# Weight-quarter sums moved between the stages of a decoder layer, a drain of GpSimd behind the last of them, and mLSTM scores made for two heads in turn

## The chip, the cores and the metric

The kernel runs on one core of one Trainium2 chip. The metric is the device time of one execution in microseconds, as the median of several runs, compared on the same chip with runs of the kernel before. A profile is one execution of its own, taken by the hardware profiler.

TensorE (PE, with PEld for its weight loads) multiplies, VectorE (DVE), ScalarE (ACT) and GpSimd (POOL) work on tiles, and SyncE (SP) issues nearly all transfers. Each engine takes its instructions in the order in which they stand in the program, and waits on semaphores where one needs the result of another engine. GpSimd issues transfers too: those that add to what stands at the destination.

## The reference

One decoder layer on 512 tokens of width 1024, all in float32, in three steps, each between two norms and with a residual:

```python
x = x + 0.5 * rms_norm(swiglu_ffn(rms_norm(x, norm_pre[0]), ffn1_w_in, ffn1_w_out), norm_post[0])
x = x + rms_norm(token_mixer(rms_norm(x, norm_pre[1]), ...), norm_post[1])
x = x + 0.5 * rms_norm(swiglu_ffn(rms_norm(x, norm_pre[2]), ffn2_w_in, ffn2_w_out), norm_post[2])

def swiglu_ffn(x, w_in, w_out):            # inner width 2816
    gate, up = jnp.split(x @ w_in, 2, axis=-1)
    return (jax.nn.silu(gate) * up) @ w_out
```

The token mixer makes one combined projection and runs two recurrences on its columns, an HGRN2 with four heads of 128 and an mLSTM with four heads of 64 (keys and queries) and 128 (values), each with a norm and a gate, and then an output projection. The scores of an mLSTM head are, chunk by chunk,

```python
D = jnp.where(causal, b[..., :, None] - b[..., None, :] + ic[..., None, :], -jnp.inf)
P = jnp.einsum("bhtd,bhsd->bhts", qc, kc) * jnp.exp(D - m_t[..., None])
```

## The kernel before

Every product of the large matrices is made of three products of rounded parts: a weight tile `raw` of 512 KB is loaded by SP (`load`, L242), ScalarE writes its rounded part and VectorE the rest (`split`, L279 and L281), and TensorE multiplies high by high, high by low and low by high. Both FFNs save products with a scheme of seven products of quarters in place of eight (`prod` and `after` for the first matrix, `quartered` and `common` for the second). The scheme needs sums of quarters of the weights. For the first matrix they are made on chip (L295). For 13 of the 22 blocks of the second matrix they are made in DRAM ahead of time, and loaded like weights.

Such a sum is made by `sums_ahead(f, h, k2)`, for FFN `f` ("f1" or "f2"), output half `h` and block `k2`, in steps of a generator. The first step puts three copies on SP (L868 to L870), behind the latest weight load. The next three steps issue one accumulating DMA each from GpSimd (L873). Each of these three reads what the one before wrote, so it waits for its landing. `make_sums` starts one new sum, if `sums_due` has left any, and moves each open one a step on. It is called from places in the other work:

- first FFN: sums of "f1", in `ffn_in`, at every fifth product behind the fourteenth, and in the first half of `ffn_out`
- mixers: the eight sums of "f2", half 0 (blocks 2 to 9), at the four `job_f` of the convolution's columns and at each weight pull of the `job_t` of "hi" and "mv", twelve calls
- second FFN: the five sums of "f2", half 1 (blocks 2, 4, 3, 6, 8), in `ffn_in` at every tenth product behind the fourteenth, and in the first half of `ffn_out` behind each second block (`if half == 0 and n % 2`)

In `ffn_out` each output half runs over eleven blocks; between the halves `post0` takes the squares of half 0 and its statistics, some of them on GpSimd (`rms`, L437).

The mixers interleave the recurrences with the big projections: a queue of jobs (`job_f`, `job_t`, `job_rows`) holds the matmuls of the projections, and `fill(n)` takes n pieces from it between the small steps. The order of each engine's instructions is fixed when the program is built; a scheduler may move instructions within the bounds of their needs. In the built program GpSimd's DMAs of the eight mixer sums stand in one run, ahead of the clearing of the mLSTM state (L1548) and of the four causal selects (L1515).

`mlstm_scores` makes the scores of the four heads. For a head, `mlstm_head` takes the row maxima by a matmul with a selector (`neg_m`, L1489), VectorE and ScalarE make the decay `e` (L1511 to L1514), GpSimd sets to zero what isn't causal (L1515), TensorE multiplies keys and queries, four chunks into one PSUM bank (L1523), and VectorE multiplies both into `pT` (L1525). Heads 0 and 2 lie in the lower 64 rows of their tile, heads 1 and 3 in the upper ones. Behind them come two more `neg_m`, transposes of the keys (L1570) and the state updates (L1585). PSUM has eight banks; four of them hold the running projection.

At the end of the program each engine closes with a drain, and a barrier of all engines ends the kernel (L1861).

Of the kernel before, what the change touches and what calls it, by code (L numbers as in the profile page):

```python
# [11 lines left out]
ALU = mybir.AluOpType  # L12
# [6 lines left out]
NT = T // P  # L19
# [9 lines left out]
NH = 4  # L29
# [55 lines left out]
PLACES, LATER = {2: 1, 4: 2, 6: 0, 8: 3}, {7: (2, 3)}  # L85

AGAIN, ROWS = (10,), (18, 19, 20, 21)
EVERY = 5, 10

# [25 lines left out]
class Layer:  # L117
# [663 lines left out]

    def ffn_in(self):

        self.sums_due("f2" if self.second else "f1", (1,) if self.second else (0, 1))
        for n, (p, t) in enumerate(ORDER2[len(HEADS2) :] if self.second else ORDER[len(HEADS) :]):
            if n > 14 and n % EVERY[self.second] == 0:
                self.make_sums()
            with self.behind(*(self.c22 if p == "p3" and self.second else ())):
                self.feed()
            self.c22 = []  # L790
            self.lag()
            self.prod(p, t)
            self.after(p, t)
            if t == PAIRS - 1 and p in ("p3", "p7"):
                self.hs.append(self.h_tile(len(self.hs)))
        self.feed()
        self.lag()
# [64 lines left out]
    def sums_ahead(self, f, h, k2):  # L862

        nc, to = self.nc, self.sums_of[f, h, k2]
        w = (self.ffn1_w_out, self.ffn2_w_out)[f == "f2"][0]
        q = w[k2 * 2 * P : (k2 + 1) * 2 * P, h * 512 : (h + 1) * 512].rearrange("(k p) (c f) -> p k c f", p=P, f=QUARTER)
        with self.behind(self.loaded):
            nc.sync.dma_start(to[:, 0], q[:, 0, 1])  # L868
            nc.sync.dma_start(to[:, 1], q[:, 1, 0])
            nc.sync.dma_start(to[:, 2:], q[:, 1])  # L870
        yield
        for a, b, v in ((0, 2, q[:, 0, :1].broadcast_to([P, 2, QUARTER])), (2, 3, to[:, :1]), (3, 4, to[:, 2:3])):
            nc.gpsimd.dma_start(to[:, a:b], v, accum_op=ALU.add)  # L873
            yield

    def sums_due(self, f, halves):
        self.ahead, self.making = deque(k for k in self.sums_of if k[0] == f and k[1] in halves), []

    def make_sums(self):

# [4 lines left out]
    def ffn_out(self, gpost_row, scale, after, trans, head):  # L885
# [81 lines left out]

        with self.behind(*([self.loaded] if self.second else [])):
            g = self.gain("gpost", gpost_row)
        n = 0  # L970
        for half in range(2):
            C = [[self.ps() for _ in range(2)] for _ in range(2)]
            M, T, left = None, None, len(QUARTERED[half])
            for m, k2 in enumerate(OUT[half][: PAIRS - LAST * half]):
# [24 lines left out]
                    self.after("p4", PAIRS - 1)  # L999
                self.lag()  # L1000
            if half == 0:
                ys = [self.post0(pieces(C, i), g, scale) for i in range(NT)]
                self.holes()
        ws = []
# [41 lines left out]
    def job_f(self, name, then):  # L1046

        w, ps = self.pull(), self.ps()
        if name[0] == "c":
            self.make_sums()  # L1050
        for k in range(ND):
            self.in_k(ps, w, k, [(0, HALF), (HALF, T)])
# [374 lines left out]
    def job_rows(self):  # L1427

        ps = self.ps()[:100]
        for k in range(ND):  # L1430
            for n in range(2):
                for m in range(2):
# [71 lines left out]
    def mlstm_head(self, h):  # L1504

        nc = self.nc
# [14 lines left out]
        for c in range(NT):  # L1521
            s = slice(c * P, (c + 1) * P)
            nc.tensor.matmul(sc[:, s], self.qk[o : o + 64, 2 + h // 2, s], self.qk[o : o + 64, h // 2, s], start=True, stop=True)  # L1523
        yield
        nc.vector.scalar_tensor_tensor(self.pT[:, h, :], sc, 0.125, e, op0=ALU.mult, op1=ALU.mult)  # L1525
        yield

    def mlstm_scores(self, mc):
# [2 lines left out]
        self.nend = mc.tile([P, NH, NT], F32, name="nend")  # L1531
        self.pT = mc.tile([P, NH, T], F32, name="pT")
        H = [self.mlstm_head(h) for h in range(NH)]
        next(H[0])
        for h in range(NH):
            if h + 1 < NH:
                next(H[h + 1])
            self.fill(3)
            next(H[h])
            next(H[h])  # L1540
        w = mc.tile([P, NT, NH], F32, name="w")
        nc.vector.tensor_tensor(w, self.aT, self.nend.rearrange("p h c -> p c h"), op=ALU.add)
        nc.scalar.activation(w, w, AF.Exp)
# [127 lines left out]
    def mixer(self):  # L1671
        nc, tc = self.nc, self.tc
        self.got, self.jobs = set(), deque()
        self.sums_due("f2", (0,))
        with tc.tile_pool(name="ma", bufs=1) as ma:
            self.vh = ma.tile([P, NT, NH, P], F32, name="vh")
            self.vm = ma.tile([P, NT, NH, 129], F32, name="vm")
# [187 lines left out]
```

## Time and profile before

| | |
|---|---|
| median of 3 runs | 937.68 us (935.62 to 940.22) |
| profiled execution | 936.0 us, its span 934.3 us |
| granted TensorE clock | 0.998 |
| busy: PE, DVE, ACT, POOL | 922.8, 759.2, 521.5, 179.5 us |
| first FFN, mixers, second FFN | about 0 to 340, 340 to 600, 600 to 934 us |
| mixer sums on GpSimd | 394.95 to 484.44 us |

In the rows below a time is in us from the start of the span. A row of a timeline gives start, duration, engine, line, operation, what is written and read, the number of instructions merged, and in brackets how long the engine stood idle before it and what ended that. PEld is the weight load of TensorE, which runs beside the matmuls. A row of the waits reads: engine, tile, line, what it waited for, us in total, times, longest. A row of a window gives its bounds and length, then the busy us and the number of instructions of PE, PEld, DVE, ACT and POOL, the granted clock, the busy share of the DMA engines and GB/s. The busy time of a pipelined matmul overlaps the next one, so the number of matmuls in a window tells more than its busy time.

### The profile page before, as it was taken

To read this page: it belongs to the slowest core of one execution; us is meant where nothing else is said; L and a number is where in the kernel's file an instruction comes from. 1 tells how busy PE (TensorE), PEld (TensorE's weight loads), DVE (VectorE), ACT (ScalarE), POOL (GpSimd) and SP (SyncE) were. 2 spreads that over 40 slices of the span, in tenths; PEclk is the share of its full clock that TensorE was granted. 3 is DMA by queue.
4 is the path that set the end of the run, shared out by engine and by line. 5 is a ranking of instruction groups with operands and counts; after the bars stand their busy time and mean duration, and the time that the engine had idled before them with its cause. 6 is when DMAs were issued, how large, how long until landed. Compare 5 with 4: busy or idle time off the path is not lost.

```text
span 934.3 us, 18295 instructions
## 1 busy us (share of the span) xinstructions
PE 922.8 (99%) x7435; PEld 887.7 (95%) x7435; DVE 759.2 (81%) x980; ACT 521.5 (56%) x751; POOL 179.5 (19%) x250
## 2 busy tenths in 40 slices
PE   9999999999999999999999999999999999999996
PEld 7999999999999999998888887899999999999996
DVE  6899988889887786698766555799899889988883
ACT  7646455557566457956523345594445545756641
POOL 3531112211111045222230310313010010100001
PEclk9999999999999999999999999999999999999999
DMA  9255778766996234477742125253376556467522
GB/s 315 70 152 143 187 206 194 193 147 160 241 276 215 81 98 123 121 176 160 170 87 63 45 90 175 88 166 93 97 192 171 150 159 198 132 193 224 175 74 91
DMA packets 116494, 142.28 MB, mean 152 GB/s; under 512 B 7189, under 2 KB 89657, under 8 KB 116410
## 3 DMA queue, kind: packets, MB, share of 16 engines
q1 hardware_dynamic: 101562, 126.95, 43.8%
q0 software_dynamic: 14560, 13.64, 11.2%
q8 instruction: 58, 0.95, 0.4%
q10 hardware_dynamic: 288, 0.52, 0.2%
q14 instruction: 26, 0.21, 0.1%
HBM read 138.99 MB, written 29.36 MB: 180 GB/s over the span
## 4 chain that ended last, share of the span: by engine, by line
PE 54%; DVE 5%; issue 2%; DMA 2%; POOL 1%; ACT 1%; DVEq 0%; POOLq 0%; ACTq 0%
PE ps L602 14%; PE ps L928 7%; PE ps L532 6%; PE ps L920 5%; PE ps L185 5%; PE ps L187 5%; PE ps L186 5%; DVE w L281 2%; PE ps L1342 2%; DMA raw<-in_ffn_w_in_dram 2%; DVE raw L295 1%; PE ps L347 1%; POOL raw L295 1%; PE ps L542 1%; PE ps L1523 0%
## 5 line engine op out<-in xcount | busy, mean ns | idle before, releaser
L279 ACT CAST w<-raw 128x1024 fp32r<-128x1024 f32 x244 | 249.6, 1029 | 195.8 <-PE ps L602 85.5
L281 DVE TENSOR_TENSOR w<-raw,w 128x1024 fp32r<-128x1024 f32 x244 | 297.5, 1222 | 32.8 <-ACT w L279 31.5
L602 PE MATMUL ps<-xq,w 128*128 128x256 f32 x2016 | 237.3, 277 | 0.0
L602 PEld LDWEIGHTS ps<-xq,w 128*128 128x128 f32 x2016 | 232.9, 188 | 0.1
L602 PE MATMUL ps<-sq,w 128*128 128x256 f32 x1512 | 178.2, 276 | 2.2 <-DVE ps L621 1.8
L602 PEld LDWEIGHTS ps<-sq,w 128*128 128x128 f32 x1512 | 174.3, 188 | 3.2 <-issue 2.0
L295 DVE TENSOR_TENSOR raw<-raw,raw 128x1024 f32<-128x1024 f32 x72 | 89.8, 1251 | 11.8 <-DMA raw<-in_ffn_w_in_dram 10.3
L920 PE MATMUL ps<-w,hs 128*128 128x256 f32 x768 | 91.2, 276 | 0.0
L920 PEld LDWEIGHTS ps<-w,hs 128*128 128x128 f32 x768 | 88.9, 188 | 0.0
L185 PE MATMUL ps<-w,xq 128*128 128x512 f32 x192 | 78.0, 407 | 0.1
L928 PE MATMUL ps<-w,hs 128*128 128x256 f32 x624 | 75.0, 276 | 0.0
L186 PE MATMUL ps<-w,xq 128*128 128x512 f32 x192 | 74.9, 391 | 0.0
L187 PE MATMUL ps<-w,xq 128*128 128x512 f32 x192 | 74.8, 391 | 0.0
L928 PEld LDWEIGHTS ps<-w,hs 128*128 128x128 f32 x624 | 72.7, 188 | 0.0
L532 PE MATMUL ps<-xq,w 128*128 128x256 f32 x480 | 55.7, 277 | 0.0
L532 PEld LDWEIGHTS ps<-xq,w 128*128 128x128 f32 x480 | 54.9, 188 | 0.5 <-issue 0.5
L814 ACT CAST hs<-hf 128x1024 fp32r<-128x1024 f32 x34 | 35.8, 1053 | 34.2 <-PE ps L928 22.3
L815 DVE TENSOR_TENSOR hs<-hf,hs 128x1024 fp32r<-128x1024 f32 x34 | 41.5, 1221 | 11.9 <-ACT hs L814 11.5
L873 POOL DMA_DIRECT2D f1sums<-f1sums x26 | 22.8, 879 | 111.7 <-DMA f1sums<-in_ffn_w_out_dram 53.1
L185 PEld LDWEIGHTS ps<-w,xq 128*128 128x128 f32 x192 | 36.1, 188 | 8.5 <-issue 0.9
L187 PEld LDWEIGHTS ps<-w,xq 128*128 128x128 f32 x192 | 36.0, 188 | 8.1 <-DVE xq L354 0.3
L873 POOL DMA_DIRECT2D f2sums<-in_ffn_w_out_dram x13 | 17.3, 1333 | 137.3 <-DMA f2sums<-in_ffn_w_out_dram 137.3
(262 smaller groups left out, 1201.6 us busy)
## 6 DMA issues: line engine op xcount, KB each, us to landing
raw<-in_ffn_w_in_dram SPq DMA_DIRECT2D x98, 512.0 KB, 4.9
raw<-in_ffn_w_out_dram SPq DMA_DIRECT2D x44, 512.0 KB, 4.5
raw<-in_w_mix_in_dram SPq DMA_DIRECT2D x28, 512.0 KB, 4.1
raw<-f1sums SPq DMA_DIRECT2D x13, 512.0 KB, 7.5
raw<-f2sums SPq DMA_DIRECT2D x13, 512.0 KB, 4.5
raw<-in_w_mix_out_dram SPq DMA_DIRECT2D x8, 512.0 KB, 4.3
f1sums<-in_ffn_w_out_dram SPq DMA_DIRECT2D x26, 128.0 KB, 4.4
f1sums<-in_ffn_w_out_dram SPq DMA_DIRECT2D x13, 256.0 KB, 5.5
```

What stands on the lines that cost most here:

```text
L185: mm(ps, sh, mh, start=start, stop=False, **kw)
L186: mm(ps, sh, ml, start=False, stop=False, **kw)
L187: mm(ps, sl, mh, start=False, stop=stop, **kw)
L279: nc.scalar.copy(hi, raw)
L281: self.low = nc.vector.tensor_tensor(lo, raw, hi.bitcast(F32), op=ALU.subtract)
L295: (nc.vector if late else nc.gpsimd).tensor_tensor(o, o, c, op=ALU.add)
L532: mm(ps[:, u0:u1], w[:, a, k, :], self.xop(k, b, u0, u1), start=k + n + m == 0, stop=k == ND - 1 and n == 2, skip_group_check=True,)
L602: self.nc.tensor.matmul(ps[:, c], wb[b][:, k, v], left[d][:, k, :], start=first and a + n + k == 0, stop=n == 2 and k == KH - 1, skip_grou ...
L815: self.nc.vector.tensor_tensor(lo, src, hi.bitcast(F32), op=ALU.subtract)
L873: nc.gpsimd.dma_start(to[:, a:b], v, accum_op=ALU.add)
L920: mm(out, a[kk][:, i * P : (i + 1) * P], w[:, b, kk, QUARTER * v : QUARTER * (v + 1)], start=begin and c == kk == n == 0, stop=kk == 1 and ...
L928: mm(ps[:, QUARTER * c : QUARTER * (c + 1)], A[a][:, c], B[b], start=begin and c == n == 0, stop=n == 2, skip_group_check=True,)
```

## The change

Five edits go together:

- `sums_due` takes a number instead of halves. The mixers now make the first ten sums of "f2": half 0's eight, and blocks 2 and 4 of half 1.
- `job_rows` gets a call of `make_sums` of its own, so that there are thirteen calls in the mixers. (`job_f`'s test for the convolution's columns is written out and selects the same four jobs.)
- the second FFN's `ffn_in` makes no sums. The last three (half 1, blocks 3, 6, 8) are started in the first half of its `ffn_out`, at the calls that stood there already.
- behind the first half of the second `ffn_out`, after the issue of the last accumulating DMA, GpSimd gets a drain. In the built program it stands between that DMA and the statistics of `post0`.
- the mLSTM heads go in pairs: both `neg_m` and decays, pieces of the projection, the next pair's `neg_m` and decays, pieces again, and then the score matmuls of the two heads in turn, one chunk of the one and one of the other. The number of pieces between the steps is the same in all. All four `e` are alive at once, and the score matmuls of the first pair stand behind the decays of the second.

In the built program the thirty DMAs of the ten mixer sums stand on GpSimd ahead of the clearing of the state and of the four selects. The first `pT` stands on VectorE behind the decays of all four heads, the fifth `neg_m` on TensorE waits for the first `pT`, and the transposes behind it for the second, for their PSUM banks.

```diff
--- before.py
+++ after.py
@@ -85,7 +85,7 @@
 PLACES, LATER = {2: 1, 4: 2, 6: 0, 8: 3}, {7: (2, 3)}
 
 AGAIN, ROWS = (10,), (18, 19, 20, 21)
-EVERY = 5, 10
+EVERY, AHEAD = 5, 10
 
 
 
@@ -781,9 +781,10 @@
 
     def ffn_in(self):
 
-        self.sums_due("f2" if self.second else "f1", (1,) if self.second else (0, 1))
+        if not self.second:
+            self.sums_due("f1")
         for n, (p, t) in enumerate(ORDER2[len(HEADS2) :] if self.second else ORDER[len(HEADS) :]):
-            if n > 14 and n % EVERY[self.second] == 0:
+            if n > 14 and n % EVERY == 0 and not self.second:
                 self.make_sums()
             with self.behind(*(self.c22 if p == "p3" and self.second else ())):
                 self.feed()
@@ -870,11 +871,11 @@
             nc.sync.dma_start(to[:, 2:], q[:, 1])
         yield
         for a, b, v in ((0, 2, q[:, 0, :1].broadcast_to([P, 2, QUARTER])), (2, 3, to[:, :1]), (3, 4, to[:, 2:3])):
-            nc.gpsimd.dma_start(to[:, a:b], v, accum_op=ALU.add)
+            self.summed = nc.gpsimd.dma_start(to[:, a:b], v, accum_op=ALU.add)
             yield
 
-    def sums_due(self, f, halves):
-        self.ahead, self.making = deque(k for k in self.sums_of if k[0] == f and k[1] in halves), []
+    def sums_due(self, f, n=None, done=0):
+        self.ahead, self.making = deque([k for k in self.sums_of if k[0] == f][done:n]), []
 
     def make_sums(self):
 
@@ -967,6 +968,8 @@
 
         with self.behind(*([self.loaded] if self.second else [])):
             g = self.gain("gpost", gpost_row)
+        if self.second:
+            self.sums_due("f2", done=AHEAD)
         n = 0
         for half in range(2):
             C = [[self.ps() for _ in range(2)] for _ in range(2)]
@@ -999,6 +1002,9 @@
                     self.after("p4", PAIRS - 1)
                 self.lag()
             if half == 0:
+                if self.second:
+                    with self.behind(self.summed):
+                        nc.gpsimd.drain()
                 ys = [self.post0(pieces(C, i), g, scale) for i in range(NT)]
                 self.holes()
         ws = []
@@ -1046,7 +1052,7 @@
     def job_f(self, name, then):
 
         w, ps = self.pull(), self.ps()
-        if name[0] == "c":
+        if name in ("conv0", "conv1", "conv2", "conv3"):
             self.make_sums()
         for k in range(ND):
             self.in_k(ps, w, k, [(0, HALF), (HALF, T)])
@@ -1427,6 +1433,7 @@
     def job_rows(self):
 
         ps = self.ps()[:100]
+        self.make_sums()
         for k in range(ND):
             for n in range(2):
                 for m in range(2):
@@ -1521,7 +1528,7 @@
         for c in range(NT):
             s = slice(c * P, (c + 1) * P)
             nc.tensor.matmul(sc[:, s], self.qk[o : o + 64, 2 + h // 2, s], self.qk[o : o + 64, h // 2, s], start=True, stop=True)
-        yield
+            yield
         nc.vector.scalar_tensor_tensor(self.pT[:, h, :], sc, 0.125, e, op0=ALU.mult, op1=ALU.mult)
         yield
 
@@ -1531,13 +1538,17 @@
         self.nend = mc.tile([P, NH, NT], F32, name="nend")
         self.pT = mc.tile([P, NH, T], F32, name="pT")
         H = [self.mlstm_head(h) for h in range(NH)]
+
         next(H[0])
-        for h in range(NH):
-            if h + 1 < NH:
+        next(H[1])
+        for h in range(0, NH, 2):
+            self.fill(3)
+            for g in H[h + 2 : h + 4]:
+                next(g)
+            self.fill(3)
+            for _ in range(NT + 1):
+                next(H[h])
                 next(H[h + 1])
-            self.fill(3)
-            next(H[h])
-            next(H[h])
         w = mc.tile([P, NT, NH], F32, name="w")
         nc.vector.tensor_tensor(w, self.aT, self.nend.rearrange("p h c -> p c h"), op=ALU.add)
         nc.scalar.activation(w, w, AF.Exp)
@@ -1671,7 +1682,7 @@
     def mixer(self):
         nc, tc = self.nc, self.tc
         self.got, self.jobs = set(), deque()
-        self.sums_due("f2", (0,))
+        self.sums_due("f2", AHEAD)
         with tc.tile_pool(name="ma", bufs=1) as ma:
             self.vh = ma.tile([P, NT, NH, P], F32, name="vh")
             self.vm = ma.tile([P, NT, NH, 129], F32, name="vm")
```

## The prediction

> **What bounds the kernel now.** I read the page first, then the windows, then who waits on TensorE, then the GpSimd rows of the mixers, because the change moves work on that queue.
>
> ```profile
> span 934.3 us, 18295 instructions
> PE 922.8 (99%) x7435; PEld 887.7 (95%) x7435; DVE 759.2 (81%) x980; ACT 521.5 (56%) x751; POOL 179.5 (19%) x250
> ```
> ```profile
> 760.00:800.00 40.00, 38.10 (x334) 37.74 (x333) 38.37 (x42) 20.89 (x27) 4.50 (x5) 1.00 0.58 160
> 800.00:840.00 40.00, 40.00 (x356) 40.00 (x354) 36.45 (x49) 25.97 (x35) 2.84 (x3) 1.00 0.60 172
> ```
> ```profile
> PE ps L602 <- DVE ps L621: 1.8, 1, 1.8
> ```
> TensorE sets the time: busy 922.8 of 934.3 us at full granted clock. A full stretch of 40 us in the second FFN holds 356 matmuls; the one from 760 to 800 holds 334, 22 x 0.112 = 2.5 us short, and TensorE's only wait of any size there is the 1.8 us above. So little can be won by removing stalls. Anything that makes TensorE wait anew is paid in full.
>
> **Part 1: two sums move into the mixers, and a call is added.** A sum is three accumulating DMAs on GpSimd, here a, b, c (L873), each waiting for the landing of the one before. GpSimd works in order. These are its rows from the fourth sum of the mixers' eight to the work behind them:
>
> ```profile
> 429.35 0.81 POOL L873 DMA_DIRECT2D f2sums<-f2sums  x1 [2.57 <-DMA f2sums<-f2sums]
> 429.87 1.49 POOL L873 DMA_DIRECT2D f2sums<-in_ffn_w_out_dram  x1
> 436.90 0.85 POOL L873 DMA_DIRECT2D f2sums<-f2sums  x1 [5.54 <-DMA f2sums<-in_ffn_w_out_dram]
> 437.43 1.52 POOL L873 DMA_DIRECT2D f2sums<-in_ffn_w_out_dram  x1
> 440.34 0.85 POOL L873 DMA_DIRECT2D f2sums<-f2sums  x1 [1.39 <-DMA f2sums<-f2sums]
> 450.11 1.49 POOL L873 DMA_DIRECT2D f2sums<-in_ffn_w_out_dram  x1
> 462.68 0.81 POOL L873 DMA_DIRECT2D f2sums<-f2sums  x1 [2.72 <-DMA f2sums<-f2sums]
> 474.60 1.48 POOL L873 DMA_DIRECT2D f2sums<-in_ffn_w_out_dram  x1
> 481.00 0.85 POOL L873 DMA_DIRECT2D f2sums<-f2sums  x1 [4.92 <-DMA f2sums<-in_ffn_w_out_dram]
> 484.44 0.94 POOL L873 DMA_DIRECT2D f2sums<-f2sums  x1 [2.59 <-ACT vm L1696]
> 485.42 1.40 POOL L1548 MEMSET C<- 128x1548 f32 x1
> 486.77 0.83 POOL L1515 TENSOR_SCALAR_AFFINE_SELECT e<-e 128x512 f32<-128x512 f32 x1
> ```
> From 429 on GpSimd goes from sum to sum without a pause (a follows the previous c within about 0.5 us). The last c issues at 484.44, and the clearing of C and the causal selects of the mLSTM heads (L1515) come directly behind it. The queue is just in time now. With ten sums, all thirty DMAs still stand ahead of these selects, so two more chains delay them.
>
> The new call in job_rows starts block 6 one call earlier. The built order has a of block 6 directly behind a of block 5, and a of block 7 directly behind c of block 5. So block 7 starts after 440.34 + 0.85, about 441.4 with its neighbours' issue, and not at 450.11. From its a to the c of block 9 the rows take 484.44 - 450.11 = 34.3 us: 475.7. Then two chains like the last one (474.60 to 484.44, 9.84 us, and 0.5 us to go from one to the next): 475.7 + 0.5 + 9.84 + 0.5 + 9.84 = 496.4 for the last c. The first select ends 486.77 + 0.83 - 484.44 = 3.16 us behind it: 499.6.
>
> Who waits: the first pT (L1525, VectorE), which frees the PSUM bank that the fifth neg_m matmul (L1489) takes; the second pT frees the bank of the transposes (L1570).
>
> ```profile
> 488.60 0.68 DVE L1525 SCALAR_TENSOR_TENSOR pT<-ps,e 128x512 f32<-128x512 f32 x1
> 497.36 0.49 PE L1489 MATMUL ps<-nm,selr 36*128 36x512 f32 x1
> 497.89 0.55 PE L1570 MATMUL ps<-ident,qk 128*128 128x128 f32 x3
> ```
> pT ends at 499.6 + 0.1 + 0.7 = 500.4, so L1489 runs 3.0 us later than at 497.36. The next select and pT are 0.8 us behind, so the transposes come at 501.1, 3.2 us later than 497.89. Behind the pT's VectorE holds a weight split, dq, kw and qdm; they run while TensorE does the following nine matmuls, and I add nothing for them. **+3.2 us.**
>
> Ends: all five sums from block 7 on at 9.84 + 0.5 put the last c at 441.4 + 5 x 10.34 - 0.5 = 492.6, and L1489 0.8 us earlier than now: -0.8. The two new chains as slow as block 7's (450.11 to 462.68, 12.6 us) make +8.7. I take the rows nearest in time, those of the last chain.
>
> [...]
>
> **Part 2: scores of two heads in turn.**
>
> ```profile
> 486.51 1.16 PE L1523 MATMUL ps<-qk 64*128 64x128 f32 x8
> 487.40 0.19 PEld L1489 LDWEIGHTS ps<-nm,selr 36*128 36x128 f32 x1
> ```
> ```profile
> PEld ps L1523 <- issue: 1.1, 3, 0.4
> ```
> A head's eight score matmuls take 487.40 - 486.51 = 0.9 us. The same 32 instructions run, in two groups for four, and TensorE leaves the big matmuls once less for this stage; each departure shows about 0.35 us of issue (1.1 in 3): 0.4 to 0.7 us saved. Whether two heads on different halves of the rows overlap no row shows: 0 to 1.8 us (two groups of 1.8 halved). It all lies ahead of the L1489 matmul that waits for GpSimd, so TensorE only comes earlier to the same wait. **0**; it is worth 0.7 to 2.5 us only if the selects are early.
>
> **Part 3: no sums in the second FFN's ffn_in.**
>
> ```profile
> 749.31 0.51 SPq L868 DMA_DIRECT2D f2sums<-in_ffn_w_out_dram  x1
> 754.47 1.17 POOL L873 DMA_DIRECT2D f2sums<-in_ffn_w_out_dram  x1 [22.61 <-DMA f2sums<-in_ffn_w_out_dram]
> 759.96 1.23 DVE L295 TENSOR_TENSOR raw<-raw,raw 128x1024 f32<-128x1024 f32 x1 [3.50 <-DMA raw<-in_ffn_w_in_dram]
> 771.80 2.98 PE L602 MATMUL ps<-sq,w 128*128 128x256 f32 x24 [1.80 <-DVE ps L621]
> ```
> ```profile
> 753.62 6.21 DMA raw<-in_ffn_w_in_dram
> ```
> ```profile
> raw<-in_ffn_w_in_dram SPq DMA_DIRECT2D x98, 512.0 KB, 4.9
> ```
> The first fence is from the timeline, the second from the chain of waits, the third from the page's list of DMAs. The weight load of 753.62 shares the DMA engines with a sum's copies and its a; it lands after 6.2 us where the median is 4.9, VectorE idles 3.5 us, runs full until 771.6 and makes TensorE wait. Without the sum the load lands 1.3 us earlier, and the wait shrinks by about as much. With the smaller losses by the other sums: **-1.5 us** (ends 0, if VectorE is short anyway, and -2.3).
>
> **Part 4: three sums in ffn_out's first half, then the drain.** SP's copies follow the loads of 815.40, 831.32 and 840.35:
>
> ```profile
> 815.40 0.42 SPq L158 DMA_DIRECT2D gpost<-in_norm_post_dram  x1
> 831.32 0.33 SPq L242 DMA_DIRECT2D raw<-f2sums  x1
> 834.55 0.38 SPq L242 DMA_DIRECT2D raw<-in_ffn_w_out_dram  x1
> 840.35 0.33 SPq L242 DMA_DIRECT2D raw<-f2sums  x1
> 844.01 0.38 SPq L242 DMA_DIRECT2D raw<-in_ffn_w_out_dram  x1
> ```
> ```profile
> 811.79 1.17 POOL L873 DMA_DIRECT2D f2sums<-in_ffn_w_out_dram  x1 [16.71 <-DMA f2sums<-in_ffn_w_out_dram]
> 823.31 0.81 POOL L873 DMA_DIRECT2D f2sums<-f2sums  x1 [5.97 <-DMA f2sums<-f2sums]
> 870.20 0.19 POOL L437 TENSOR_SCALAR col<-col 128x1 f32<-128x1 f32 x1 [46.08 <-ACT junk L436]
> ```
> Three issues on SP take about 1.8 us and fit into the gaps between loads (831.7 to 834.55, 840.7 to 844.01). A sum there takes 811.79 to 823.31, 11.5 us from a to c: a of the third at about 849, its c at 860. The drain stands behind it. GpSimd isn't asked for anything until 870.20, so ten microseconds cover it. **0**; if it waits for the landing (6 us, as the row of 823.31 waited) and then takes 5.5, it ends near 872, the statistics of post0 come late, and the banks of half 0 with them: up to +3.
>
> **Part 5: the end.**
>
> The first two rows give the number of closing drains, their least, median and longest ns, and where they lie; the third is from the chain of waits.
>
> ```profile
> L1861 POOLq DRAIN x3: 34/102/5506, 928.0 to 934.0; - x3
> L1861 SPq DRAIN x3: 7/7/7, 932.2 to 933.8; - x3
> ```
> ```profile
> 927.98 0.60 POOLq L1861
> ```
> GpSimd's closing drain lasts 5.5 us from 928.0, to 933.5; SP has seen the last store land by 932.2. So the drain ends last, by 1.3 us. The next one, with no DMA before it, takes 0.1 us. If the long one is the settling of GpSimd's DMAs, the new drain has done it and SP ends the kernel: **-1.3 us** (or 0, if it is a fixed cost).
>
> Sum: +3.2 - 1.5 - 1.3 = +0.4 us on the profiled execution's 936.0 us (span 934.3). That execution lies 1.7 us under the median of the runs, 937.68, so I forecast 938 us for the median.
>
> **Rivals.** Half a per cent, 4.7 us, is about what a measurement of this kernel can tell from no change.
> - *The GpSimd queue costs more (slower).* If the last c issues after 500.7, part 1 costs over 7.5 us and the gains of 2.8 don't hold it. At the +8.7 end the sum is +5.9: 943.6; without the gains of parts 3 and 5, 946. For it: block 7's chain of 12.6 us. Against it: the last one's 9.84.
> - *The queue is in time and the heads overlap (faster).* Last c by 492: part 1 gives -0.8, the overlap up to 1.5 more, parts 3 and 5 2.8: -3.6 to -5.1, 932.6 to 934. [...]
> - *The drain doesn't do what it says*: the closing one stays at 5.5 us, or the new one delays post0: +1.7 to +4.7, 939.4 to 942.4.
>
> **How the numbers follow.** The forecast case (a wait of 1 to 6 us in the mixers, roughly paid for by parts 3 and 5) gets 0.62, its own range 935 to 941; the slow queue 0.20; the fast case 0.10, of which most passes 0.5%; the drain 0.08, within 0.5%. Hence faster 0.08, same 0.72, slower 0.20. The range reaches from the fast case to the slow queue's nearer part: 933 to 945.
>
> **What would show it.** In the changed profile: the last f2sums DMA of the mixers near 496 and L1515's counterpart behind it; a TensorE wait of 3 to 5 us ahead of the fifth neg_m matmul; no f2sums between 600 and 780 and TensorE's wait of 1.8 us gone or under 0.7; a drain of about 5 us near 861; a closing GpSimd drain under 1 us, and the end 1 us behind SP's. It would be wrong if the ten chains end before 492 or after 501, if the three late sums hold up a load, or if the drain reaches past 870.

## The result, and the profile after

The changed kernel takes 940.26 us (median of 22 runs, 938.24 to 948.21), the kernel before on the same chip 937.1 us (22 runs, 935.36 to 941.41). The ratio is **1.0036, with a 95% interval of 1.0023 to 1.005**: slower by about 3.3 us, within the 0.5% that I had called "same". The forecast was 938.0 us in a range of 933 to 945.

The head of the page of the changed kernel, and the whole list of what TensorE waited for (engine, tile, line, releaser; us in total, times, longest):

```profile
span 937.9 us, 18290 instructions
PE 923.5 (98%) x7435; PEld 888.1 (95%) x7435; DVE 758.2 (81%) x980; ACT 521.2 (56%) x751; POOL 180.9 (19%) x250
```
```profile
PE ps L1496 <- DVE pT L1532: 4.3, 1, 4.3
PE ps L181 <- POOL ident masks.py:199: 1.6, 1, 1.6
PE ps L929 <- DVE y L474: 1.4, 1, 1.4
PE ps L602 <- DVE ps L621: 0.4, 1, 0.4
```

The profiled execution is 3.6 us longer than that of before (937.9 against 934.3). Two waits are new: 4.3 us for the first pT in the mixers (L1496 was L1489, L1532 was L1525), and 1.4 us for y behind the first half of the second ffn_out (L929 was L928). One has shrunk: that of ffn_in was 1.8 us (L602). The 1.6 us at L181 lie at the program's start, and other runs below have them too.

**The mixers.** GpSimd's timeline (L874 issues the sums, L1522 makes the selects), then TensorE's:

```profile
493.58 0.85 POOL L874 DMA_DIRECT2D f2sums<-f2sums  x1 [6.11 <-DMA f2sums<-in_ffn_w_out_dram]
496.97 0.81 POOL L874 DMA_DIRECT2D f2sums<-f2sums  x1 [2.53 <-DMA f2sums<-f2sums]
497.82 1.39 POOL L1559 MEMSET C<- 128x1548 f32 x1
499.17 2.42 POOL L1522 TENSOR_SCALAR_AFFINE_SELECT e<-e 128x512 f32<-128x512 f32 x4
```
```profile
489.71 1.16 PE L1530 MATMUL ps<-qk 64*128 64x128 f32 x16
495.11 1.16 PE L1530 MATMUL ps<-qk 64*128 64x128 f32 x16
500.61 0.79 PE L1496 MATMUL ps<-nm,selr 36*128 36x512 f32 x1 [4.34 <-DVE pT L1532]
505.74 0.50 PE L1496 MATMUL ps<-nm,selr 36*128 36x512 f32 x1
515.38 0.83 PE L1646 MATMUL ps<-vm,pT 128*128 128x129 f32 x6
```

The same places of TensorE before:

```profile
500.44 0.50 PE L1489 MATMUL ps<-nm,selr 36*128 36x512 f32 x1
510.06 1.06 PE L1635 MATMUL ps<-vm,pT 128*128 128x129 f32 x8
```

The last sum's DMA is issued at 496.97, the selects come behind it, and the fifth neg_m runs at 500.61, 3.25 us later than the 497.36 of before. Two things were not foreseen. TensorE reached that wait early, at 496.3, because 16 score matmuls took the 1.16 us that 8 took before. And the sixth neg_m is 5.3 us late, not 3.25, with the values behind it (515.38 against 510.06). The windows of the changed kernel show why; the last three numbers of a row are the granted clock, the DMA share and GB/s, and behind the length stand PE's busy us with its number of matmuls:

```profile
496.00:500.00 4.00, 0.27 (x6) 0.08 (x2) 0.14 (x1) 0.00 (x0) 2.99 (x4) 0.82 0.26 37
500.00:504.00 4.00, 3.39 (x9) 2.57 (x10) 4.00 (x8) 0.59 (x1) 1.59 (x3) 0.50 0.06 9
504.00:506.00 2.00, 2.00 (x6) 1.24 (x5) 1.43 (x4) 0.62 (x2) 0.00 (x0) 0.66 0.71 245
506.00:508.00 2.00, 2.00 (x11) 1.58 (x11) 1.09 (x3) 1.14 (x2) 0.00 (x0) 1.00 0.00 0
```

The idle time cost TensorE its clock: by the clock records of the trace it was granted half from 498.54 to 505.37, so that 500 to 504 holds 9 matmuls, and only from 506 on does a window of 2 us hold 11 again. The profile is no exception: over a whole execution, the mean granted clock of all 22 timed runs is 0.997 or less (median 0.995), where before's is 0.998 in the profile and in the median of its timed runs. A fall of 6.83 us to one half takes 0.0036 off such a mean.

**The second ffn_out and the end.** From the timelines of GpSimd, ScalarE and TensorE, and the drains (count; least, median and longest ns; first and last start):

```profile
825.68 1.25 POOL L874 DMA_DIRECT2D f2sums<-in_ffn_w_out_dram  x1 [176.24 <-DMA f2sums<-in_ffn_w_out_dram]
840.26 0.81 POOL L874 DMA_DIRECT2D f2sums<-f2sums  x1 [5.76 <-DMA f2sums<-f2sums]
857.92 1.48 POOL L874 DMA_DIRECT2D f2sums<-in_ffn_w_out_dram  x1
873.91 0.81 POOL L874 DMA_DIRECT2D f2sums<-f2sums  x1 [6.06 <-DMA f2sums<-f2sums]
882.02 0.19 POOL L437 TENSOR_SCALAR col<-col 128x1 f32<-128x1 f32 x1 [7.30 <-issue]
882.24 0.38 ACT L436 ACTIVATE junk<-ps 128x256 f32<-128x256 f32 x1 [5.59 <-POOL col L437]
883.23 1.65 PE L929 MATMUL ps<-w,hs 128*128 128x256 f32 x12 [1.37 <-DVE y L474]
```
```profile
L1007 POOLq DRAIN  x1: 8014/8014/8014, 873.9 to 873.9; - x1
```
```profile
L1872 POOLq DRAIN  x3: 34/102/657, 932.9 to 937.7; - x3
L1872 SPq DRAIN  x3: 7/7/7, 937.1 to 937.4; - x3
```

A sum takes 14.6 us (825.68 to 840.26) to 16.0 us (857.92 to 873.91) here. The last DMA goes out at 873.91, and the drain behind it ends at 881.9. The first statistic of post0 waits for it, ScalarE's seventh square waits for it (882.24, released by L437), y waits for the square, and TensorE for y. At the end GpSimd's closing drain lasts 0.66 us in place of 5.5, and SP is last: 937.1 to 937.9 is 0.8 us, where 932.2 to 934.3 was 2.1 us.

The sum of the profile, read from where TensorE stands in the timelines of before and after: the second FFN's first matmul starts at 600.15 and 605.49 (+5.3, of which 0.3 was there at the first neg_m, 483.61 and 483.91), its ffn_out's first at 813.14 and 816.42 (-2.1 in ffn_in, more than the wait alone shows), its last matmul ends at 926.86 and 931.80 (+1.7, most of it the wait for y), and the end behind that is 1.3 shorter. Together that is +3.6, as measured.

### The profile page after: what moved, and what is told of

Read it like the earlier page. It is cut to its first block, busy times and chain, and to the rows that moved or that the text cites. A ratio compares the mean times of both kernels' runs of the same rounds, so it can differ in the third digit from the quotient of the medians.

```text
span 937.9 us, 18290 instructions
## 1 busy us (share of the span) xinstructions
PE 923.5 (98%) x7435; PEld 888.1 (95%) x7435; DVE 758.2 (81%) x980; ACT 521.2 (56%) x751; POOL 180.9 (19%) x250
## 5 line engine op out<-in xcount | busy, mean ns | idle before, releaser
L602 PE MATMUL ps<-xq,w 128*128 128x256 f32 x2016 | 237.1, 277 | 0.0
L602 PEld LDWEIGHTS ps<-xq,w 128*128 128x128 f32 x2016 | 232.9, 188 | 0.0
L602 PE MATMUL ps<-sq,w 128*128 128x256 f32 x1512 | 178.0, 276 | 0.7 <-DVE ps L621 0.4
L602 PEld LDWEIGHTS ps<-sq,w 128*128 128x128 f32 x1512 | 174.2, 188 | 1.4 <-ACT ps L653 0.9
L295 DVE TENSOR_TENSOR raw<-raw,raw 128x1024 f32<-128x1024 f32 x72 | 89.8, 1251 | 7.4 <-DMA raw<-in_ffn_w_in_dram 5.9
L929 PE MATMUL ps<-w,hs 128*128 128x256 f32 x624 | 75.2, 276 | 1.4 <-DVE y L474 1.4
L929 PEld LDWEIGHTS ps<-w,hs 128*128 128x128 f32 x624 | 72.7, 188 | 1.6 <-DVE y L474 1.6
L874 POOL DMA_DIRECT2D f2sums<-in_ffn_w_out_dram x13 | 18.2, 1460 | 191.2 <-DMA f2sums<-in_ffn_w_out_dram 190.9
L874 POOL DMA_DIRECT2D f1sums<-f1sums x26 | 22.4, 860 | 113.8 <-DMA f1sums<-in_ffn_w_out_dram 57.7
```

The costliest lines, as they stand in the source:

```text
L295: (nc.vector if late else nc.gpsimd).tensor_tensor(o, o, c, op=ALU.add)
L602: self.nc.tensor.matmul(ps[:, c], wb[b][:, k, v], left[d][:, k, :], start=first and a + n + k == 0, stop=n == 2 and k == KH - 1, skip_grou ...
L874: self.summed = nc.gpsimd.dma_start(to[:, a:b], v, accum_op=ALU.add)
L929: mm(ps[:, QUARTER * c : QUARTER * (c + 1)], A[a][:, c], B[b], start=begin and c == n == 0, stop=n == 2, skip_group_check=True,)
```

## Experiments

All were timed beside the kernel before. Where a run of mine is compared with the changed kernel, that kernel's 1.0036 is the measure; its interval (1.0023 to 1.005) comes on top of the run's own, so such a difference of under about 2 us is not clear of the noise.

### The scores in turn, alone

On the kernel before, the change's two hunks on the heads (`yield` moved into the chunk loop, and the loop over pairs):

```diff
         next(H[0])
-        for h in range(NH):
-            if h + 1 < NH:
-                next(H[h + 1])
-            self.fill(3)
-            next(H[h])
-            next(H[h])
+        next(H[1])
+        for h in range(0, NH, 2):
+            self.fill(3)
+            for g in H[h + 2 : h + 4]:
+                next(g)
+            self.fill(3)
+            for _ in range(NT + 1):
+                next(H[h])
+                next(H[h + 1])
```

> The kernel before with the scores of two heads in turn and nothing else (sums and GpSimd's drains as before). The selects on GpSimd end by 490 us, as before, so nothing holds TensorE up behind the scores. Theory (row halves overlap, and the gain was swallowed in the changed kernel by the wait for GpSimd): the two groups of 16 score matmuls take 0.9 us each in place of 1.8, and one departure from the big matmuls falls away: 1.5 to 2.5 us faster than before, ratio 0.9973 to 0.9984. Rival (the turn-taking is worth nothing, what was saved on TensorE was hidden anyway or the first pT, now behind four decays, comes too late): within 0.5 us of before, ratio 0.9995 to 1.0005.

Measured: 935.85 us, ratio 0.9974 (0.9964 to 0.9985), 2.4 us faster. TensorE has no wait for pT, and sixteen score matmuls take the 1.16 us that eight took:

```profile
492.32 1.16 PE L1523 MATMUL ps<-qk 64*128 64x128 f32 x16
```

The theory holds: in the medians the turn-taking is worth 2.4 us (1.4 to 3.4 by the interval) where the selects are in time. In the profile the stage from the first neg_m to the first matmul of the values takes 24.72 us (486.52 to 511.24), where before took 26.45 (483.61 to 510.06): 1.7 us, and the same in four later runs whose selects are in time. The row of 16 matmuls in the 1.16 us of 8 shows the two heads side by side.

### The heads apart again, in the changed kernel

The same hunks the other way round, all else as changed.

> The changed kernel with the heads' scores one after the other again, all else as changed, so that ten sums stand ahead of the selects. Theory (the new order also lets TensorE run further ahead of the late selects): the score matmuls of the third head take the PSUM bank of the first, so TensorE waits there, at 493.5, for the first pT at about 500.4: some 7 us, in place of 4.3 us at the fifth neg_m; the granted clock falls as well. 3 to 5 us slower than the changed kernel, ratio to before 1.007 to 1.009. Rival (the scores' order is worth nothing while GpSimd is late): as the changed kernel, ratio 1.003 to 1.004. Second rival (TensorE idles less, since it comes later to the wait, and keeps its clock): 1.5 to 2.5 us faster than the changed kernel, ratio 1.001 to 1.002.

Measured: 944.11 us, ratio 1.0071 (1.0052 to 1.009), and this from TensorE's timeline:

```profile
502.48 2.07 PE L1530 MATMUL ps<-qk 64*128 64x128 f32 x8 [9.05 <-DVE pT L1532]
```

The third head's scores wait 9.05 us for the bank of the first. With the old order of the scores the whole change costs twice as much. The turn-taking wins back about 3.3 us (1.0071 to 1.0036), chiefly because it lets TensorE run further before it needs a pT: the wait is 4.3 us in place of 9.05. Of the 4.7 us between the two waits, 2.8 are TensorE's earlier arrival (493.43 against 496.27); the other 1.9 come from the chain of sums, whose last DMA went out at 498.85 in this execution, not at 496.97.

### The drain alone

```diff
             if half == 0:
+                if self.second:
+                    with self.behind(self.summed):
+                        nc.gpsimd.drain()
                 ys = [...]
```

> The kernel before with the drain of GpSimd behind the first half of the second ffn_out and nothing else. The last sum's c is issued at about 823 us here, and GpSimd is asked for nothing before 870. Theory (the long closing drain is the settling of GpSimd's DMAs, and the new drain does it unseen): a drain of 5 to 9 us behind about 824, over by 835; the closing one under 1 us; 1.0 to 1.3 us faster, ratio 0.9986 to 0.9990. Rival (a drain of GpSimd at the end costs 5.5 us whatever stood before): no change, ratio 0.9997 to 1.0003. Second rival (a drain costs the later work of GpSimd something by itself): slower by 1 to 2 us, ratio 1.001 to 1.002.

Measured: 936.44 us, ratio 0.9981 (0.9969 to 0.9992). The drains of this run, the new one (L1004) and the closing ones:

```profile
L1004 POOLq DRAIN  x1: 9213/9213/9213, 824.9 to 824.9; - x1
```
```profile
L1864 POOLq DRAIN  x3: 34/102/656, 929.7 to 934.4; - x3
```

The new drain lies hidden from 824.9 to 834.1, and the closing one is short. The gain of 1.8 us is a little over the theory's, whose 1.0 to 1.3 us lie within the interval. The profiled execution doesn't show it in its span (934.7 us), since it lost time elsewhere:

```profile
PE ps L602 <- DVE ps L621: 2.2, 1, 2.2
```

Behind this wait in ffn_in the clock was at one half for 3.41 us, from 772.01. The kernel before, with a wait of 1.8 us at the same place, kept its clock.

### The drain behind post0

Two tries in the changed kernel. In the first, the drain's two lines were put behind `ys = [...]`:

> The changed kernel with the drain behind the statistics of post0 in place of ahead of them. Theory (the drain, which ended at 881.9 and held the first statistics from 870.2 to 882.0, cost the 1.4 us that TensorE waited for y): that wait goes, the closing drain stays under 1 us, 1.2 to 1.6 us faster than the changed kernel, ratio to before 1.0015 to 1.0025. Rival (GpSimd's queue would have been late anyway, since the last c is issued only at 873.9): 0 to 0.5 us faster, ratio 1.003 to 1.0036, the wait for y still there.

In the built program the drain stayed directly behind the last DMA, since nothing but `self.summed` held it. So this run is the changed kernel once more: 941.2 us, ratio 1.0033 (1.0022 to 1.0045). Its profile still tells something:

```profile
L1008 POOLq DRAIN  x1: 6777/6777/6777, 876.1 to 876.1; - x1
```

The drain ended at 882.9, and yet TensorE's list of waits has none for y: its mixers had cost it 1.2 us more (a wait of 5.5 us for pT), so it came to y later. Of the seven profiles that have the drain at this place behind three late sums, only that of the changed kernel shows a wait for y. In the second try the drain was tied to the last statistic:

```diff
-            nc.gpsimd.tensor_scalar(m, ss, s2 / D, b, op0=ALU.mult, op1=ALU.add)
+            self.stat = nc.gpsimd.tensor_scalar(m, ss, s2 / D, b, op0=ALU.mult, op1=ALU.add)
...
+                if self.second:
+                    with self.behind(self.stat):
+                        nc.gpsimd.drain()
```

> The changed kernel with the drain held behind the last of post0's eight statistics (in the built program it now stands behind them). Theory (the drain cost 0 to 1.5 us in the changed kernel, by how late TensorE is there when it ends): TensorE never waits for y, the drain of 5.5 us or a little more lies between 880 and 890, the closing drain stays under 1 us: 0.5 to 1.5 us faster than the changed kernel, ratio to before 1.002 to 1.003. Rival (the long drain only follows directly on a DMA; behind other work it does not settle them): the closing drain is 5.5 us again, and the time is that of the changed kernel or 1 us more, ratio 1.0035 to 1.005.

```profile
L1008 POOLq DRAIN  x1: 5227/5227/5227, 879.2 to 879.2; - x1
```
```profile
L1872 POOLq DRAIN  x3: 34/102/656, 932.6 to 937.3; - x3
```

Measured: 940.34 us, ratio 1.0034 (1.0018 to 1.0051). The wait for y is gone and the closing drain is short, as the theory says, but the time isn't better than the changed kernel's 1.0036 by anything that can be measured. The ratio lies between the theory's range and the rival's. What the place of the drain is worth in the mean is too small for these medians to show.

### The wait filled with other work

Six more pieces of the projection ahead of the fifth neg_m, taken from the same queue of jobs:

```diff
         dcs = []
+        self.fill(6)
         for p in range(2):
             nm = self.neg_m(4 + p)
```

> The changed kernel with six more pieces of the projection (some 5 us of matmuls, taken from the same queue of jobs, so that later places get fewer) between the second pair's scores and the fifth neg_m. All ten sums stay ahead of the selects. Theory (what the late selects cost is TensorE's idle time of 4.3 us and the half clock that follows it, and nothing else): TensorE comes to the fifth neg_m at about 501, when the first pT is done, doesn't wait over 0.5 us, and its clock stays at 1.00: 5 to 6.5 us faster than the changed kernel, if the later places don't lack the pieces, ratio to before 0.996 to 0.9985. Rival (the late selects put the whole stage off, since the key transposes and the states come later all the same, or the pieces are missed later): the wait comes back behind it, 0 to 2 us faster than the changed kernel, ratio 1.0015 to 1.0035. Second rival (the clock drop comes from something else than the idle time): it is there without the wait, and 4 us are gained, ratio 0.9985 to 1.0.

Measured: 935.91 us, ratio 0.9986 (0.9967 to 1.0005), some 4.7 us faster than the changed kernel, at the edge of the theory's range. GpSimd's last sum DMA of the mixers, the first wait of size on TensorE, and the windows:

```profile
496.49 0.81 POOL L874 DMA_DIRECT2D f2sums<-f2sums  x1 [2.53 <-DMA f2sums<-f2sums]
```
```profile
PE ps L1597 <- DVE C L1607: 1.2, 1, 1.2
```
```profile
500.00:504.00 4.00, 3.94 (x20) 2.58 (x18) 4.00 (x8) 0.59 (x1) 1.10 (x2) 1.00 0.15 23
```

The selects are as late as in the changed kernel, TensorE has work all the same, and the clock stays at 1.00. So the cost lay in TensorE's idle time and what followed from it. It isn't all won back: a wait of 1.2 us for the states comes behind.

With three pieces in place of six:

> The changed kernel with three more pieces of the projection ahead of the fifth neg_m, in place of six. [...] Rival (any wait here halves the clock): a drop to 0.5 for 3.4 to 6.8 us, 2 to 3 us faster than the changed kernel, ratio 1.0 to 1.0015.

Measured: 938.65 us, ratio 1.0021 (1.0009 to 1.0033), 1.4 us faster than the changed kernel, which the intervals don't tell from nothing; the rival's range of 1.0 to 1.0015 doesn't hold it. The profiled execution had a late chain of sums, and shows what happens then:

```profile
500.14 0.81 POOL L874 DMA_DIRECT2D f2sums<-f2sums  x1 [2.52 <-DMA f2sums<-f2sums]
```
```profile
504.00:508.00 4.00, 4.00 (x11) 2.98 (x12) 4.00 (x10) 1.63 (x2) 0.75 (x2) 0.50 0.22 46
```

The last DMA went out at 500.14, TensorE waited 5.4 us, and the clock fell. The last of the thirty DMAs goes out between 496.5 and 500.1 in the profiles of the kernels that have them all ahead of the selects and start them at the same calls, so the cover of three pieces (TensorE is busy for 2.34 us from 496 to 500 here, for 0.27 in the changed kernel) isn't always enough. How much of the gain that six pieces bring and three don't is the clock's, this run doesn't separate.

### The clock alone

The second pair's score matmuls were made five times over into the same banks (64 instructions that add nothing):

```diff
-        for c in range(NT):
+        for c in list(range(NT)) * (5 if h > 1 else 1):
...
-            for _ in range(NT + 1):
+            for _ in range(NT * (5 if h else 1) + 1):
```

> The changed kernel with the score matmuls of the second pair of heads made five times over into the same banks (64 more instructions, the same values), so that TensorE is busy for some 3.6 us of the 4.3 us that it waits for GpSimd, and nothing else moves. Theory (a good part of the cost is the half clock that follows the idle time): the wait for the first pT shrinks to under 1 us, the clock stays at 1.00, and the same wait costs about 2 us less: 1.3 to 2.3 us faster than the changed kernel, ratio to before 1.001 to 1.0025. Rival (the clock drop costs nothing of its own, since VectorE and GpSimd set the pace of the stage behind the late selects): the time of the changed kernel, ratio 1.003 to 1.0045. Second rival (matmuls that use half of the rows in turn don't count as work for the clock): the clock falls all the same.

```profile
495.51 4.74 PE L1530 MATMUL ps<-qk 64*128 64x128 f32 x80
500.58 0.50 PE L1496 MATMUL ps<-nm,selr 36*128 36x512 f32 x1 [0.34 <-DVE pT L1532]
513.38 1.06 PE L1646 MATMUL ps<-vm,pT 128*128 128x129 f32 x8
```
```profile
500.00:504.00 4.00, 3.56 (x20) 2.31 (x16) 4.00 (x8) 0.59 (x1) 1.56 (x3) 1.00 0.05 5
```

The fifth neg_m runs at 500.58, as in the changed kernel (500.61), with nothing won on the wait itself. The clock stays at 1.00, and the first matmul of the values comes at 513.38 in place of 515.38: **2.0 us are the clock's**. The time is 937.96 us, ratio 1.0012 (0.9996 to 1.0027), where the theory gave 1.001 to 1.0025. By the ratios that is 2.2 us under the changed kernel, for matmuls that add nothing to the result; the two intervals just touch. The 2.0 us rest on the one profile. In the timed runs the clock was not always kept: the six with a mean clock of 0.998 or more took 935.1 to 937.9 us, the six with 0.995 to 0.997 took 938.1 to 941.9.

### Other places for the two sums

Eight sums ahead of the selects as before (without the call in `job_rows`), and the two further ones among the last projection ("mo") and the values of both recurrences:

```diff
-            if name in ("hi", "mv"):
+            if name in ("hi", "mv", "mo"):
                 self.make_sums()
...
+                self.sums_due("f2", AHEAD, EARLY)
                 self.jobs.append(self.job_t("mo", self.gate_mo))
...
-        self.sums_due("f2", AHEAD)
+        self.sums_due("f2", EARLY)
```

> The changed kernel with only eight sums ahead of the selects (and no call in job_rows), as before, and the two further sums among the last projection and the values of both recurrences, 525 to 600 us; the second ffn_in still makes none, the second ffn_out three. Theory (the cost of the change is that thirty DMAs stand ahead of the selects, not how many sums are made where): the wait at the fifth neg_m and the clock drop go, the scores in turn give their 2.4 us, ffn_in keeps its 1.4: 5 to 8 us faster than the changed kernel, ratio to before 0.995 to 0.998. Rival (GpSimd's norms of the values stand between the six DMAs now, and wait for their landings): a new wait of 2 to 6 us between 540 and 600, ratio 0.999 to 1.003.

Measured: 940.8 us, ratio 1.0035 (1.002 to 1.0049). The wait in the mixers has only moved. From TensorE's waits and GpSimd's timeline:

```profile
PE ps L187 <- DVE xq L354: 5.1, 1, 5.1
```
```profile
545.69 0.90 POOL L874 DMA_DIRECT2D f2sums<-f2sums  x1 [4.83 <-DMA f2sums<-f2sums]
548.14 1.03 POOL L339 TENSOR_TENSOR col<-col,nhalf 128x4 f32<-128x4 f32 x1
```

The rival's mechanism holds, at a time just over its range: the norms of the values (L339) stand behind a DMA that waits 4.83 us for a landing, and TensorE waits 5.1 us for what follows from them. The chain of waits leads from this DMA over the norms and VectorE to that wait, and the clock fell once more, for 6.83 us from 553.30.

Nine sums ahead, the tenth at the first products of the second ffn_in, and the drain behind post0:

```diff
-            if n > 14 and n % EVERY == 0 and not self.second:
+            if n in (3, 6, 9, 12) if self.second else n > 14 and n % EVERY == 0:
```

> The changed kernel with nine sums ahead of the selects in place of ten, the tenth in the first calls of the second ffn_in (at products 3, 6, 9 and 12), the last three in ffn_out, and the drain behind post0's statistics. Theory (one chain of about 10 us fewer brings the last c from 497 to 487): the first pT is there by 493, no wait at the fifth neg_m, no clock drop; the scores in turn give 2.4 us, the closing drain 1.3, and ffn_in 0 to 1.4, by where the tenth sum's DMAs lie: 5 to 8 us faster than the changed kernel, ratio to before 0.9945 to 0.998. Rival (the tenth sum holds up a weight load in ffn_in as the sums there did before): the wait of 1.8 us in ffn_in is there, at another place, ratio 0.997 to 0.999.

Measured: 939.94 us, ratio 1.0035 (1.0022 to 1.0048). The selects are in time, but from GpSimd's and ScalarE's timelines:

```profile
641.48 0.81 POOL L876 DMA_DIRECT2D f2sums<-f2sums  x1 [2.53 <-DMA f2sums<-f2sums]
642.04 2.68 POOL L295 TENSOR_TENSOR raw<-raw,raw 128x1024 f32<-128x1024 f32 x1
644.75 1.05 ACT L279 CAST w<-raw 128x1024 fp32r<-128x1024 f32 x1 [9.36 <-POOL raw L295]
```

GpSimd makes some of the first matrix's sums itself (L295). One of them stood behind the tenth sum's DMAs, and ScalarE waited 9.36 us for it. Then TensorE lost time, as windows of this run and of the changed kernel show:

```profile
660.00:680.00 20.00, 17.76 (x149) 17.16 (x147) 17.07 (x19) 8.42 (x10) 0.00 (x0) 1.00 0.29 92
```
```profile
660.00:680.00 20.00, 20.00 (x179) 20.00 (x178) 17.77 (x20) 8.15 (x9) 0.00 (x0) 1.00 0.30 96
```

From 640 to 700 us this run has 466 matmuls and the changed kernel 533. That the lost time follows from ScalarE's wait is argued from the rows, not tried. If so, it is the same fault at a third place, and not the one that the rival named.

### The gains without the cost

The turns and the drain on the kernel before, all sums in their old places:

> The kernel before with the scores in turn and the drain, and with its own places for all sums (eight ahead of the selects, two sums in the second ffn_in). Theory (the two edits act in different places, and neither touches a wait of the other): their gains add, -2.4 and -1.8 us as measured alone: 933.0 to 934.5 us, ratio 0.9945 to 0.9965. Rival (both save the same idle time, or one of them was chance): no better than the turns alone, ratio 0.997 to 0.9985.

Measured: 933.89 us, ratio 0.9966 (0.9949 to 0.9983). The gain of 3.2 us lies between the turns alone (2.4) and the sum of the two (4.2), and the interval takes in both. Whether the gains add in full stays open in the medians; in the profile the stage of the scores is 1.7 us shorter than before, and the end 1.3.

And the changed kernel with its ten sums begun earlier, at all eight jobs of the mixers' first two groups of columns, with the drain behind post0:

```diff
         w, ps = self.pull(), self.ps()
-        if name in ("conv0", "conv1", "conv2", "conv3"):
-            self.make_sums()
+        self.make_sums()
```

> The changed kernel with a call at each of the eight job_f of the mixers in place of four, so that the ten sums begin some 45 us earlier, and the drain behind post0's statistics. Theory (the late selects are a matter of when the chain of thirty DMAs starts, since it runs without a pause): the last c is issued by 488, the selects end by 491, no wait at the fifth neg_m and no clock drop, and the scores in turn, the second ffn_in without sums and the short closing drain all show: 6 to 8 us faster than the changed kernel, ratio to before 0.994 to 0.997. Rival (GpSimd is busy with the gates and masks until about 390, so the chain can't begin earlier, or the earlier waits for landings hold those up): last c at 493 or later, a wait of 1 to 4 us stays, ratio 0.998 to 1.003.

```profile
475.38 0.81 POOL L874 DMA_DIRECT2D f2sums<-f2sums  x1 [3.21 <-DMA f2sums<-f2sums]
486.82 0.83 POOL L1521 TENSOR_SCALAR_AFFINE_SELECT e<-e 128x512 f32<-128x512 f32 x1 [6.30 <-ACT e L1520]
```
```profile
PE ps L602 <- DVE ps L621: 0.9, 1, 0.9
```

Measured: **932.35 us, ratio 0.9945 (0.9933 to 0.9957)**, 5.2 us faster than the kernel before and, by the ratios, some 8.5 us faster than the changed one. The last DMA goes out 21.6 us earlier (475.38 against 496.97), and the first select now waits for ScalarE, no longer for the queue. This version beats both kernels: the change as a whole pays once the chain of sums starts early enough. In its profile the stage of the scores is 1.7 us shorter than before, the second ffn_in 1.4 us, and the end 1.3 us. Against the turns and the drain alone (0.9966) it gains 2 us, and the two intervals overlap, so the medians don't show for certain that moving the sums is worth its trouble.

## Why the prediction was right, and where its parts were not

The time came out: 940.26 us in a range of 933 to 945, and within 0.5% of before. The likeliest case was the one that happened, a wait in the mixers partly paid for by ffn_in and the end. The forecast of 938.0 lay 2.3 us low, and these steps made it so:

- *Part 1, the queue on GpSimd.* Right within 0.6 us: the last DMA at 496.97 (forecast 496.4), the fifth neg_m 3.25 us late (3.0). Some of that is luck: the last two chains took 9.0 and 11.0 us (476.47 to 485.46, 485.99 to 496.97) where each was put at 9.84, and other profiles have the last DMA at up to 500.14. Wrong behind it: "they run while TensorE does the following nine matmuls, and I add nothing for them". Nothing was to be added for VectorE, but the stall halved the granted clock for 6.83 us. That is the term that was missing: 2.0 us, measured with the repeated scores. No row of the profile before has a fall of the clock inside the run, so no row gave it; its end bounds (-0.8 to +8.7) did hold the 5.3 us.
- *Part 2, the scores in turn.* "TensorE only comes earlier to the same wait" describes what happened, and the 0.7 to 2.5 us for selects in time came out at 2.4 in the medians and 1.7 in the profiles; the overlap of two heads, which no row showed ahead, is there in full (16 score matmuls in the 1.16 us of 8). As the value of the edit, though, 0 was wrong: without it the ten sums cost 3.3 us more (1.0071), because the old order waits for the first pT at the third head. I had set part 1's price at the fifth neg_m, a place that only part 2 made possible.
- *Part 3, ffn_in.* Forecast -1.5; TensorE's wait went from 1.8 to 0.4 us in the profiled execution. The four profiles that keep the sums there as before show waits of 1.7 to 2.2 us, the nine without any there 0 to 1.2, in the mean 0.7: -1.2. From the first matmul of the second ffn_in to the first of ffn_out the four take 213.1 us in the mean and the nine 211.5, so the whole stage gains 1.6, with "the smaller losses by the other sums" that the forecast had counted in.
- *Part 4, the three late sums and the drain.* "A sum there takes 811.79 to 823.31, 11.5 us from a to c" was too short: 14.6 to 16.0 us. The third sum's a also stood behind the second's c (857.39), so it came at 857.92 and not at 849. Its c came at 873.91 and not at 860, and the drain reached past 870, which the prediction had named as the point that would make it wrong. In the profile it cost 1.4 us, inside the bound of +3; six other profiles with the drain there show no such wait, and with the drain out of the way the median did not improve by anything measurable.
- *Part 5, the end.* Forecast -1.3, measured 1.3 in the profile, and the drain alone gave 1.8 (0.8 to 2.9) us in the medians.

Of the rivals, the slow queue did not come as described (c by 497, not after 500.7), but the stage cost 5.3 us all the same: 3.25 by the queue and 2.0 by the clock. The fast case was sound: with the queue in time, the early version reached 932.35, just under its 932.6 to 934.

## What to carry to other kernels

Price a stall at the place where the engine will wait in the new order of its instructions, and add what the idle time does to the clock behind it: here 4.3 us of idle cost 2.0 us more. Work put on an in-order queue that waits for landings is free only as long as nothing urgent stands behind it; three different places for the last sums each delayed another small job (the selects, the norms of the values, a sum of weights), and of the places tried only the earlier start was free of that.

## What the runs showed of the hardware

- *The clock falls with waits of TensorE.* In the clock records of the traces the granted clock went to one half inside the run for 6.83 us with the wait of 4.3 us in the changed kernel, and for as long with waits of 4.3 us (the drain tied to the last statistic), 5.1 (the two sums late), 5.4 (three pieces) and 5.5 (the first try with the drain); for 10.24 us with the 9.05 of the heads apart; and for 3.41 us with the 2.2 of the drain alone and with the tenth sum in ffn_in, where TensorE had waited 2.4 us up to 680.92 and the clock of 680 to 700 is 0.91. No such fall came with the 1.8 us of the kernel before, the 1.9 of the turns with the drain and the 1.2 with six pieces. What decides whether the clock falls, and for how long, these runs don't show.
- *A drain of GpSimd behind DMAs.* Directly behind an accumulating DMA it took 9.2 us (the drain alone), 8.0 (the changed kernel) and 6.8 (the first of the two tries behind post0); in the changed kernel it ended 3.2 us after that DMA's landing (issued at 873.91, landed 4.8 us later). Tied to the last statistic, 7.4 us behind the issue of the last DMA (871.75), it took 5.2; at the end of the kernel before, over 100 us behind the issue of the last such DMA (823.31), 5.5; with an earlier drain and no DMA between, 0.66. So in these runs the cost was paid once, by whichever drain came first.
